# The first three feature blocks behind two layer norms, taken from unnormalized rows

## Chip, cores and metric

The kernel runs on one core of a Trainium2 chip. The metric is the device time of one execution in microseconds (us), and the time of a kernel is the median of its runs. PE is TensorE's matmul stream and PEld its weight loads, DVE is VectorE, ACT is ScalarE, POOL is GpSimd, SP is SyncE, which issues the weight transfers.

## What is computed

Two transformer blocks follow each other on 256 tokens of width 1024. The change touches the two places where a layer norm stands ahead of a wide product:

```python
x = layer_norm(ALPHA * x + gate1 * mixed, ln1_g[l], ln1_b[l])
h2 = x * (1.0 + scale2) + shift2
y_ffn = peer_ffn(h2, ...)              # begins with q = h2 @ w_query, 1024 x 2048
x = layer_norm(ALPHA * x + gate2 * y_ffn, ln2_g[l], ln2_b[l])
...
hn = rms_norm_2(x, norm_mix_g[0])      # second block
gate, xr = split(hn @ w_in)            # rglru_mixer, 1024 x 2048
gate = gelu(gate)
```

`layer_norm` is `(x - mean) / sqrt(var + eps) * g + b` over the 1024 features of a token. I call the two places the first norm (ahead of the query product, line L351 from 419.76 us) and the second norm (ahead of the recurrent mixer, from 1259.79 us).

## The kernel before

Activations are held feature-major: a tile `[128, 8, 256]` has 8 chunks of 128 features, with the 256 tokens along the free dimension. Every product is made in fp32 accuracy from split operands: a value is cast to `hi` (ACT, type fp32r), and `lo = value - hi` (DVE); a product takes the three matmuls hi·hi, hi·lo and lo·hi. A weight block of 1024 x 128 arrives by a transfer of SP's queue into one of four `raw` buffers, is cast to `whi` by ACT (L234) and split to `wlo` by DVE (L235). `whi` and `wlo` come from a ring of three pairs, so the cast of block n+3 waits until the matmuls of block n are over. `K.deepen` adds a second ring of three pairs; it is not there around the first norm.

One output block of 128 features is 24 matmuls (8 chunks x 3), in the function `ws` (L279 to L281). The first three blocks behind a norm are made together by `ws_wave` (L351 to L353): 72 matmuls, ordered so that chunk k of the first block comes ahead of chunk k-1 of the second, which lets the wave begin when only the first chunks are normalized.

The class `LayerNorm` works in three steps. `pair(j, acc)` is called as each pair of chunks leaves the product ahead of the norm: it updates the residual `x` (L939), squares it (ACT), and adds up sums and sums of squares (DVE, POOL). `stats` sums over the partitions with one-column matmuls against `ones` (L965), forms the negated mean and the reciprocal deviation on 128x2 tiles (L966 to L972), and spreads each over 128 partitions by two matmuls into PSUM, `B[0]` and `B[1]` (L989). `center` and `norm` (L978, L983) then subtract and multiply two chunks at a time. Behind them the caller splits the normalized rows: at the first norm ACT makes `xhi` (L906), DVE makes `h` again in fp32 (L907) and DVE or POOL subtract (L909); ACT also writes the residual `x<-x,cols` (L912). At the second norm ACT makes `xhi` (L1286), the residual (L1289) and squares for the RMS norm (L1305), and DVE makes `xlo` (L1290) and adds the squares (L1307). `Residual.factors` turns these sums into `rsB`, the RMS factor.

The order on each engine is fixed when the program is built: a scheduler places instructions by their place in the program and by when it thinks that their inputs are ready. On the chip ACT, DVE and POOL take their lists strictly in that order.

Behind the first norm the query blocks are numbered c0 to c15. c0 to c2 are the wave, c3 is the first one by `ws`; each block's `scores` (L1052, tile `psc`) follow, from the copy `R` of the block that ACT makes (L1082). Behind the second norm the wave makes three gate blocks, and x0, x1, x2, x3 (tile `xr`) are the first blocks by `ws`; DVE takes them from PSUM (`xs`, L1389) and runs a convolution (`xc`, L1391, L1393).

Of the kernel before, what the change touches and what calls it, by code (L numbers as in the profile page):

```python
# [10 lines left out]
F32 = mybir.dt.float32  # L11
# [368 lines left out]
def new_x(k):  # L380
    hi = k.xop.tile([P, 8, T], F32R, tag="hi", name=k.nm("xhi"))
    lo = k.xop.tile([P, 8, T], F32R, tag="lo", name=k.nm("xlo"))
    return hi, lo


def setup(k):
# [11 lines left out]
    k.mod = c.tile([P, 48], F32, name="mod")  # L398
    k.skT = c.tile([P, 2, P], F32, name="skT")
# [57 lines left out]
def block1_mixers(k):  # L457
# [6 lines left out]
    def sl(name, shape, dt=F32):  # L464
        return slab.tile(shape, dt, tag="s", name=k.nm(name))
# [450 lines left out]
    return fm(hhi), fm(hlo)  # L916


class LayerNorm:
# [3 lines left out]
    def __init__(self, k, x, gate, scale, work, st):  # L923
        nc = k.nc
        self.k, self.x, self.st = k, x, st
        self.sum, self.sq, self.q = work[:, 0], work[:, 1], [work[:, 2], work[:, 3]]
        self.gate = st[:, 16:24]
        nc.vector.tensor_scalar(self.gate, gate, scale / ALPHA, None, op0=OP.mult)
# [5 lines left out]
    def pair(self, j, acc):  # L934
# [9 lines left out]
        add = nc.vector.tensor_add  # L944
        if j in (1, 2):
            add(self.sum, self.sum if j == 2 else self.two(0), self.two(j))
            nc.gpsimd.tensor_add(self.sq, self.sq, q)
            if j == 2:
                nc.gpsimd.tensor_add(self.sq[:, :T], self.sq[:, :T], self.sq[:, T:])
        S, Q = self.sum[:, :T], self.sq[:, :T]  # L950
        if j == 3:
            add(S, S, self.sum[:, T:])
            add(S, S, x[:, 6])
            with self.k.tc.issue_after(add(S, S, x[:, 7]).ins):
                add(Q, Q, q[:, :T])
            add(Q, Q, q[:, T:])

    def stats(self):
# [51 lines left out]
def peer(k, X, finish):  # L1010
# [227 lines left out]
class Residual:  # L1238
# [6 lines left out]
    def start(self):  # L1245
# [23 lines left out]
        self.ln = LayerNorm(k, self.x, k.mod[:, 40:], 1.0, wk, slab.take(24))  # L1269
# [108 lines left out]
def rglru(k, res, X):  # L1378
    nc = k.nc
    with k.tc.tile_pool(name="rg", bufs=1) as slab, k.tc.tile_pool(name="rgw", bufs=2) as work:  # L1380
# [63 lines left out]
        ps = [k.mm("gt") for _ in range(3)]  # L1444
        k.ws_wave([p[:, :T] for p in ps], X)
# [3 lines left out]
        for f in range(3):  # L1449
            gt(f, ps[f])  # L1450
# [335 lines left out]
def program(tc, A, out):  # L1786
    with ExitStack() as es:
# [24 lines left out]
```

## Time and profile before

| | |
|---|---|
| median of 3 runs | 1856.93 us (1855.01 to 1860.98) |
| profiled execution, its own time | 1854.88 us |
| span of the profile | 1853.2 us |
| busy share of PE, DVE, ACT, POOL | 97%, 76%, 51%, 13% |
| matmuls of L351 to L353 at the first norm | from 419.76 to 430.27 us |
| the same at the second norm | from 1259.79 to 1270.31 us |

The span is the profiled part of one execution; its own time is 1.7 us longer. A profile row of the timeline gives the start and the length of an instruction on an engine, and in brackets how long that engine had been idle and what released it. The granted clock is a share of TensorE's full 2.4 GHz; 0.50 is the lower level, 1.2 GHz.

### The profile page before, as it was taken

To read this page: it belongs to the slowest core of one execution; us is meant where nothing else is said; L and a number is where in the kernel's file an instruction comes from. 1 tells how busy PE (TensorE), PEld (TensorE's weight loads), DVE (VectorE), ACT (ScalarE), POOL (GpSimd) and SP (SyncE) were. 2 spreads that over 40 slices of the span, in tenths; PEclk is the share of its full clock that TensorE was granted. 3 is DMA by queue.
4 is the path that set the end of the run, shared out by engine and by line. 5 is a ranking of instruction groups with operands and counts; after the bars stand their busy time and mean duration, and the time that the engine had idled before them with its cause. 6 is when DMAs were issued, how large, how long until landed. Compare 5 with 4: busy or idle time off the path is not lost.

```text
span 1853.2 us, 36938 instructions
## 1 busy us (share of the span) xinstructions
PE 1803.7 (97%) x14795; PEld 1719.7 (93%) x14795; DVE 1400.2 (76%) x2487; ACT 945.2 (51%) x1603; POOL 248.9 (13%) x273
## 2 busy tenths in 40 slices
PE   8999999989999999999999999998899999999998
PEld 6987899989999999999999999998789999788997
DVE  6998977878898977777888765568975556876554
ACT  3776765445445444444444544457754445664443
POOL 1000230010021300000000000001722222322221
PEclk9999999999999999999999999998999999999999
DMA  9666546874566555555555665664458666216662
GB/s 361 212 211 202 161 160 212 300 239 144 164 186 188 175 180 170 163 169 164 167 169 162 197 193 183 184 203 126 126 188 289 194 185 193 81 61 201 187 187 91
DMA packets 91150, 339.61 MB, mean 183 GB/s; under 512 B 10257, under 2 KB 10433, under 8 KB 89570
## 3 DMA queue, kind: packets, MB, share of 16 engines
q1 hardware_dynamic: 87794, 322.01, 55.3%
q0 software_dynamic: 2752, 14.54, 2.3%
q8 instruction: 116, 1.90, 0.4%
q10 hardware_dynamic: 432, 0.70, 0.1%
q14 instruction: 56, 0.46, 0.1%
HBM read 335.06 MB, written 5.30 MB: 184 GB/s over the span
## 4 chain that ended last, share of the span: by engine, by line
PE 81%; DVE 7%; DMA 6%; ACT 3%; issue 2%; POOL 0%; POOLq 0%; ACTq 0%; SPq 0%; DVEq 0%
PE u L279 7%; PE pv L320 7%; PE u L280 7%; PE u L281 7%; PE pv L322 7%; PE pv L321 7%; PE md L301 5%; PE up L281 3%; PE up L280 3%; PE up L279 3%; DVE wlo L235 2%; PE g L1183 2%; PE md L322 2%; PE md L321 2%; PE md L320 2%
## 5 line engine op out<-in xcount | busy, mean ns | idle before, releaser
L234 ACT CAST whi<-raw 128x1024 fp32r<-128x1024 f32 x525 | 547.8, 1045 | 529.3 <-PE u L280 196.2
L235 DVE TENSOR_TENSOR wlo<-raw,whi 128x1024 fp32r<-128x1024 f32 x525 | 662.6, 1264 | 205.1 <-ACT whi L234 202.8
L279 PE MATMUL u<-xhi,whi 128*128 128x256 f32 x1024 | 292.5, 286 | 0.0
L280 PE MATMUL u<-xlo,whi 128*128 128x256 f32 x1024 | 289.5, 283 | 0.0
L281 PE MATMUL u<-xhi,wlo 128*128 128x256 f32 x1024 | 289.5, 283 | 0.0
L320 PE MATMUL pv<-wh,whi 128*128 128x256 f32 x1000 | 285.4, 285 | 0.0
L321 PE MATMUL pv<-wh,wlo 128*128 128x256 f32 x1000 | 282.7, 283 | 0.0
L322 PE MATMUL pv<-wl,whi 128*128 128x256 f32 x1000 | 282.7, 283 | 0.0
L280 PEld LDWEIGHTS u<-xlo,whi 128*128 128x128 f32 x1024 | 196.3, 192 | 0.0
L279 PEld LDWEIGHTS u<-xhi,whi 128*128 128x128 f32 x1024 | 196.3, 192 | 0.0
L281 PEld LDWEIGHTS u<-xhi,wlo 128*128 128x128 f32 x1024 | 196.2, 192 | 0.0
L321 PEld LDWEIGHTS pv<-wh,wlo 128*128 128x128 f32 x1000 | 191.7, 192 | 0.0
L320 PEld LDWEIGHTS pv<-wh,whi 128*128 128x128 f32 x1000 | 191.7, 192 | 0.0
L322 PEld LDWEIGHTS pv<-wl,whi 128*128 128x128 f32 x1000 | 191.6, 192 | 0.0
L357 ACT ACTIVATE wh<-P 128x256 fp32r<-128x256 f32 x128 | 53.2, 417 | 199.5 <-PE pv L321 197.9
L281 PE MATMUL up<-xhi,wlo 128*128 128x256 f32 x464 | 131.5, 283 | 0.0
L279 PE MATMUL up<-xhi,whi 128*128 128x256 f32 x464 | 131.0, 282 | 0.3 <-DVE r L1481 0.3
L280 PE MATMUL up<-xlo,whi 128*128 128x256 f32 x464 | 131.3, 283 | 0.0
L1483 POOL TENSOR_TENSOR r<-r 128x256 f32<-128x256 f32 x64 | 75.7, 1185 | 262.3 <-ACT hh L1482 262.3
L358 DVE SCALAR_TENSOR_TENSOR wl<-P,wh 128x256 fp32r<-128x256 f32 x128 | 54.3, 424 | 63.7 <-ACT wh L357 63.7
L279 PEld LDWEIGHTS up<-xhi,whi 128*128 128x128 f32 x464 | 87.7, 189 | 1.6 <-DVE r L1481 0.5
L280 PEld LDWEIGHTS up<-xlo,whi 128*128 128x128 f32 x464 | 87.4, 188 | 1.2
(601 smaller groups left out, 4411.1 us busy)
## 6 DMA issues: line engine op xcount, KB each, us to landing
raw<-in_peer_u SPq DMA_DIRECT2D x128, 512.0 KB, 3.6
raw<-in_peer_v SPq DMA_DIRECT2D x128, 512.0 KB, 3.6
raw<-in_w_up SPq DMA_DIRECT2D x64, 512.0 KB, 4.2
raw<-in_w_down SPq DMA_DIRECT2D x64, 512.0 KB, 3.9
raw<-in_w_in_a SPq DMA_DIRECT2D x33, 512.0 KB, 4.1
raw<-in_ada SPq DMA_DIRECT2D x32, 512.0 KB, 4.6
raw<-in_w_in_b SPq DMA_DIRECT2D x32, 512.0 KB, 3.7
ada<-in_ada SPq DMA_DIRECT2D x8, 1024.0 KB, 12.6
```

Source lines behind the costliest of these rows:

```text
L234: nc.scalar.copy(hi, raw)
L235: self.marks.append(nc.vector.tensor_sub(lo, raw, hi.bitcast(F32)))
L279: mm(out, hi[:, s], xh(kk), start=kk == 0, stop=False)
L280: mm(out, hi[:, s], xl(kk), start=False, stop=False)
L281: mm(out, lo[:, s], xh(kk), start=False, stop=kk == nk - 1)
L301: mm(acc[2 * tc + h], x(k)[:, s], v[:, h * 512:h * 512 + 512], start=st, stop=sp)
L320: mm(o, hi[:, s], xh(k), start=f and h == 0, stop=False)
L321: mm(o, lo[:, s], xh(k), start=False, stop=False)
L322: mm(o, hi[:, s], xl(k), start=False, stop=l and h == 1)
L357: self.nc.scalar.activation(hi, full, AF.Copy, scale=scale)
L358: self.nc.vector.scalar_tensor_tensor(lo, full, scale, hi.bitcast(F32), op0=OP.mult, op1=OP.subtract)
L1483: nc.gpsimd.tensor_mul(r, r, r)
```

## The change

The first three blocks are now multiplied from rows that are not yet normalized. `pair` also splits `x * w` into `raw` tiles (`rhi`, `rlo` at the first norm, `xhi`, `xlo` at the second), where w is the product of the gains behind the norm; two extra columns of the raw tile hold w itself and the shift b. `head` runs the 72 matmuls on these tiles, 258 columns wide (tile `hd`), and `headed` corrects each block: it copies the two extra columns of the result (tile `hw`), adds negated mean times the first of them, multiplies by the reciprocal deviation `B[1]`, and the caller adds the second. The chunk sums over the partition are no longer folded on DVE and POOL first: `stats` uses 16 one-column matmuls in place of 4. The remaining blocks (c3 onwards, x0 onwards) still use normalized rows. At the first norm `h` moves from DVE to ACT, and all four subtractions go to DVE. At the second norm the normalized rows get tiles of their own, `x0hi` and `x0lo`.

```diff
-    ln = LayerNorm(k, xt, mod[:, 16:24], 0.5, lns, lst)
+    ln = LayerNorm(k, xt, mod[:, 16:24], 0.5, lns, lst, [sl(n, [P, 8, T + 2], F32R) for n in ("rhi", "rlo")],
+                   gl[:, :8], gl[:, 8:])
...
+    ln.head(3)
     with k.tc.high_priority():
         ln.stats()
...
-        for i in range(2):
-            f = 2 * j + i
+        fs = 2 * j, 2 * j + 1
+        for f in fs:
             nc.scalar.activation(hhi[:, f], xt[:, f], AF.Identity, scale=g(f), bias=b(f))
-            nc.vector.tensor_scalar(h[:, i], xt[:, f], g(f), b(f), op0=OP.mult, op1=OP.add)
-        e = nc.gpsimd if j % 2 else nc.vector
-        e.tensor_sub(hlo[:, 2 * j:2 * j + 2], h, hhi[:, 2 * j:2 * j + 2].bitcast(F32))
+        for f in fs:
+            nc.scalar.activation(h[:, f % 2], xt[:, f], AF.Identity, scale=g(f), bias=b(f))
+        nc.vector.tensor_sub(hlo[:, 2 * j:2 * j + 2], h, hhi[:, 2 * j:2 * j + 2].bitcast(F32))
...
+        for f in (2 * j, 2 * j + 1):
+            hi, lo = [v[:, f, :T] for v in self.raw]
+            w = self.w[:, f:f + 1]
+            nc.scalar.activation(hi, x[:, f], AF.Copy, scale=w)
+            nc.vector.scalar_tensor_tensor(lo, x[:, f], w, hi.bitcast(F32), op0=OP.mult, op1=OP.subtract)
...
+    def head(self, n):
+
+        self.ps = [self.k.mm("hd") for _ in range(n)]
+        self.k.ws_wave([p[:, :T + 2] for p in self.ps], (lambda i: self.raw[0][:, i], lambda i: self.raw[1][:, i]))
+
+    def headed(self, i, tmp, nm):
+
+        nc = self.k.nc
+        if i == 0:
+            nc.scalar.copy(nm, self.B[0][:, :T])
+        ps = self.ps[i]
+        c = self.hw[:, 2 * i:2 * i + 2]
+        nc.scalar.copy(c, ps[:, T:T + 2])
+        nc.vector.scalar_tensor_tensor(tmp, nm, c[:, 0:1], ps[:, :T], op0=OP.mult, op1=OP.add)
+        nc.vector.tensor_mul(tmp, tmp, self.B[1][:, :T])
+        return c[:, 1:2]
...
-        for i, u in enumerate((self.sum, self.sq)):
-            for tc in range(2):
-                nc.tensor.matmul(ps[:, i * 2 + tc:i * 2 + tc + 1], u[:, tc * P:tc * P + P], k.ones, start=True, stop=True)
+        q = self.q[1]
+        parts = [[self.sum[:, :T], self.sum[:, T:], self.x[:, 6], self.x[:, 7]],
+                 [self.sq[:, :T], self.sq[:, T:], q[:, :T], q[:, T:]]]
+        n = 0
+        for b in range(4):
+            for i in range(2):
+                for tc in range(2):
+                    nc.tensor.matmul(ps[:, i * 2 + tc:i * 2 + tc + 1], parts[i][b][:, tc * P:tc * P + P], k.ones,
+                                     start=n == 0, stop=n == 15)
+                    n += 1
...
+    nm = sub(T)
     for c in range(16):
+        q = qT[c % 2]
         if c > 2:
...
-        nc.scalar.copy(qT[c % 2], pq[c][:, :T])
+            nc.scalar.copy(q, ps[:, :T])
+        else:
+            nc.scalar.activation(q, q, AF.Identity, bias=head.headed(c, q, nm))
...
         for f in range(3):
-            gt(f, ps[f])
+            c = res.ln.headed(f, gate[:, f], res.ln.sum[:, :T])
+            nc.vector.scalar_tensor_tensor(gate[:, f], gate[:, f], c, res.rsB, op0=OP.add, op1=OP.mult)
```

The change moves instructions on every engine. The first place is ACT's list at the first norm, from the square root of the deviation (L971 before, L1000 now) to the first casts of query weights; `whi_4931` before and `whi_4970` now belong to block c3, `x<-x,cols` is the residual. Before:

```order
L971 ACTIVATE lnst<-lnst 128x2
L906 ACTIVATE xhi_4778<-x_3917,gl 128x256 x2
L912 ACTIVATE x_3917<-x_3917,cols 128x256 x2
...
L912 ACTIVATE x_3917<-x_3917,cols 128x256 x2
L234 CAST whi_4931<-raw_4929 128x1024
L234 CAST whi_4937<-raw_4935 128x1024
L234 CAST whi_4943<-raw_4941 128x1024
L1082 COPY R<-q_4842 128x256
```

and of the change, on the same engine at the same place:

```order
L1000 ACTIVATE lnst<-lnst 128x2
L909 ACTIVATE xhi_4882<-x_3918,gl 128x256 x2
L911 ACTIVATE h_4887<-x_3918,gl 128x256 x2
...
L915 ACTIVATE x_3918<-x_3918,cols 128x256 x8
L976 COPY hw<-hd_4777 128x2
L976 COPY hw<-hd_4778 128x2
L976 COPY hw<-hd_4779 128x2
L234 CAST whi_4970<-raw_4968 128x1024
L234 CAST whi_4976<-raw_4974 128x1024
L234 CAST whi_4982<-raw_4980 128x1024
L973 COPY R<-lnB_4853 128x256
L234 CAST whi_4988<-raw_4986 128x1024
L1113 ACTIVATE R<-R,hw 128x256 x2
```

Between the root and the cast for c3 stood 16 activations of 128x256, and 24 and three small copies stand there now; the rows `R` of c0 and c1, which the scores need, stand behind the cast for c6.

The second place is ACT's list at the second norm, from the root (L971, L1000) to the first normalized chunks; `whi_16050` before is the weight of a later block (x4), and now `whi_16100` is that of x0 and `whi_16130` that of x4. Before:

```order
L971 ACTIVATE res<-res 128x2
L234 CAST whi_16050<-raw_16048 128x1024
L1286 ACTIVATE xhi_15859<-res 128x256 x2
L1289 ACTIVATE res<-res,cols 128x256 x2
L1286 ACTIVATE xhi_15859<-res 128x256
```

and of the change:

```order
L1000 ACTIVATE res<-res 128x2
L976 COPY hw<-hd_15906 128x2
L234 CAST whi_16100<-raw_16098 128x1024
L234 CAST whi_16130<-raw_16128 128x1024
L1318 ACTIVATE x0hi<-res 128x256 x2
L1321 ACTIVATE res<-res,cols 128x256 x2
```

A copy from the first block of the product and a second weight cast now stand ahead of the first normalized chunk.

The third place is DVE's list at the second norm, from the negated mean (L966, L995) to the reciprocal; `wlo` is a weight split, `xlo_13681` is `lo` of the raw rows. Before:

```order
L966 TENSOR_SCALAR res<-lns_15841 128x2
L968 TENSOR_TENSOR res<-res 128x2
L969 SCALAR_TENSOR_TENSOR res<-lns_15841,res 128x2
L970 TENSOR_SCALAR res<-res 128x2
L972 RECIPROCAL res<-res 128x2
```

and of the change:

```order
L995 TENSOR_SCALAR res<-lns_15981 128x2
L959 SCALAR_TENSOR_TENSOR xlo_13681<-res,xhi_13680 128x256
L997 TENSOR_TENSOR res<-res 128x2
L959 SCALAR_TENSOR_TENSOR xlo_13681<-res,xhi_13680 128x256
L998 SCALAR_TENSOR_TENSOR res<-lns_15981,res 128x2
L235 TENSOR_TENSOR wlo_16119<-raw_16116,whi_16118 128x1024
L999 TENSOR_SCALAR res<-res 128x2
L1001 RECIPROCAL res<-res 128x2
```

Two splits of raw rows and one weight split have come between the mean and the deviation.

## Rows read from the trace of the kernel before

**Rows 1.** The page: span, and the chain that ended last by engine.

```profile
span 1853.2 us, 36938 instructions
...
PE 81%; DVE 7%; DMA 6%; ACT 3%; issue 2%; POOL 0%; POOLq 0%; ACTq 0%; SPq 0%; DVEq 0%
```

**Rows 2.** Stretches at the first norm: length, busy time by engine, clock, DMA.

```profile
410.90:414.00 3.10, 0.00 (x0) 0.00 (x1) 3.03 (x7) 0.75 (x2) 1.97 (x2) 0.86 0.01 3
...
420.00:422.00 2.00, 2.00 (x9) 1.81 (x10) 2.00 (x5) 2.00 (x5) 0.00 (x0) 0.50 0.00 0
422.00:424.00 2.00, 2.00 (x13) 2.00 (x13) 2.00 (x5) 1.90 (x5) 1.33 (x2) 0.65 0.00 0
...
440.00:445.00 5.00, 5.00 (x44) 5.00 (x44) 5.00 (x21) 1.79 (x4) 0.00 (x0) 1.00 0.55 189
```

**Rows 3.** Timeline of PE at the first norm.

```profile
410.60 0.28 PE L322 MATMUL wo<-xlo,w 128*128 128x256 f32 x1
...
414.00 1.94 PE L965 MATMUL lns<-ones,lns 128*128 128x1 f32 x8 [3.12 <-DVE lns L954]
...
419.76 0.58 PE L351 MATMUL q<-xhi,whi 128*128 128x256 f32 x1 [1.32 <-ACT xhi L906]
...
430.15 0.28 PE L353 MATMUL q<-xlo,whi 128*128 128x256 f32 x1
430.27 0.28 PE L279 MATMUL q<-xhi,whi 128*128 128x256 f32 x1
...
431.03 0.39 PE L281 MATMUL q<-xhi,wlo 128*128 128x256 f32 x1 [0.36 <-DVE wlo L235]
...
441.85 0.61 PE L1052 MATMUL psc<-skT,R 128*128 128x128 f32 x4
```

**Rows 4.** Timeline of ACT at the first norm.

```profile
419.11 1.09 ACT L906 ACTIVATE xhi<-x,gl 128x256 fp32r<-128x256 f32 x2 [2.14 <-DVE x L983]
...
426.22 1.08 ACT L912 ACTIVATE x<-x,cols 128x256 f32<-128x256 f32 x2
428.67 3.08 ACT L234 CAST whi<-raw 128x1024 fp32r<-128x1024 f32 x3 [1.37 <-PE q L353]
```

**Rows 5.** Timeline of POOL and DVE at the first norm.

```profile
410.70 1.38 POOL L947 TENSOR_TENSOR lns<-lns 128x512 f32<-128x512 f32 x1 [0.29 <-ACT lns L943]
411.00 1.37 DVE L952 TENSOR_TENSOR lns<-lns 128x256 f32<-128x256 f32 x1
...
413.08 0.41 DVE L953 TENSOR_TENSOR lns<-lns,x 128x256 f32<-128x256 f32 x1
...
415.98 0.16 DVE L966 TENSOR_SCALAR lnst<-lns 128x2 f32<-128x2 f32 x1 [1.17 <-PE lns L965]
...
418.66 0.75 DVE L983 TENSOR_TENSOR x<-x,lnB 128x256 f32<-128x256 f32 x2
```

**Rows 6.** Timeline of PE at the second norm.

```profile
1248.63 0.28 PE L322 MATMUL pv<-wl,ahead 128*128 128x256 f32 x1
...
1259.79 0.58 PE L351 MATMUL gt<-xhi,whi 128*128 128x256 f32 x1 [2.05 <-ACT xhi L1286]
...
1270.31 0.95 PE L1316 MATMUL rs<-ones,res 128*128 128x1 f32 x8
```

**Rows 7.** Timeline of ACT at the second norm.

```profile
1259.13 1.09 ACT L1286 ACTIVATE xhi<-res 128x256 fp32r<-128x256 f32 x2
...
1268.71 0.63 ACT L1305 ACTIVATE res<-res 128x512 f32<-128x512 f32 x1
```

**Rows 8.** Timeline of DVE behind the second norm.

```profile
1256.29 0.17 DVE L972 RECIPROCAL res<-res 128x2 f32<-128x2 f32 x1 [0.27 <-ACT res L971]
...
1275.87 0.42 DVE L1389 TENSOR_TENSOR xs<-xr,res 128x256 f32<-128x256 f32 x1
```

**Rows 9.** Stretches in the recurrent mixer, columns as in rows 2.

```profile
1288.00:1292.00 4.00, 4.00 (x36) 4.00 (x35) 3.01 (x5) 3.22 (x6) 3.69 (x5) 1.00 0.48 135
...
1296.00:1300.00 4.00, 4.00 (x36) 4.00 (x35) 4.00 (x5) 2.31 (x5) 2.88 (x3) 1.00 0.50 149
...
1304.00:1308.00 4.00, 0.41 (x2) 0.21 (x2) 4.00 (x6) 1.90 (x4) 2.33 (x3) 0.93 0.37 130
```

More of the change, by code (lines that the diff above doesn't have):

```diff
@@ L377, in fm, with new_x @@
     return lambda k: t[:, k, :]
[L380 to L383, printed above, removed]
+def new_x(k, wide=False):
+    x = [k.xop.tile([P, 8, T + 2], F32R, tag=n, name=k.nm("x" + n)) for n in ("hi", "lo")]
+    return x if wide else [v[:, :, :T] for v in x]
 def setup(k):
@@ L915, in block1_mixers, with __init__ @@
     es.close()
-    return fm(hhi), fm(hlo)
+    return ln, (fm(hhi), fm(hlo))
 class LayerNorm:
-    def __init__(self, k, x, gate, scale, work, st):
+    def __init__(self, k, x, gate, scale, work, st, raw, w, b):
         nc = k.nc
+        self.hw = k.hw
         self.k, self.x, self.st = k, x, st
@@ L927, in __init__ @@
         self.gate = st[:, 16:24]
+        self.raw, self.w = raw, w
+        hi, lo = raw
+        for c, v in ((T, w), (T + 1, b)):
+            nc.scalar.copy(hi[:, :, c], v)
+            nc.vector.tensor_sub(lo[:, :, c], v, hi[:, :, c].bitcast(F32))
         nc.vector.tensor_scalar(self.gate, gate, scale / ALPHA, None, op0=OP.mult)
@@ L943, in pair @@
             nc.scalar.activation(q, self.two(j), AF.Square)
-        add = nc.vector.tensor_add
+        for f in (2 * j, 2 * j + 1):
[3 more added lines that the diff above has]
+            nc.vector.scalar_tensor_tensor(lo, x[:, f], w, hi.bitcast(F32), op0=OP.mult, op1=OP.subtract)
         if j in (1, 2):
-            add(self.sum, self.sum if j == 2 else self.two(0), self.two(j))
+            nc.vector.tensor_add(self.sum, self.sum if j == 2 else self.two(0), self.two(j))
             nc.gpsimd.tensor_add(self.sq, self.sq, q)
[L948 to L956, printed above, removed]
+    def head(self, n):
[11 more added lines that the diff above has]
+        return c[:, 1:2]
     def stats(self):
@@ L1007, in take, with peer @@
         return a
-def peer(k, X, finish):
+def peer(k, head, X, finish):
     nc, A = k.nc, k.A
@@ L1075, in peer @@
     top = gen_top()
-    pq = [k.mm("q") for _ in range(3)]
-    k.ws_wave([ps[:, :T] for ps in pq], X)
+    nm = sub(T)
     for c in range(16):
+        q = qT[c % 2]
         if c > 2:
-            pq.append(k.mm("q"))
-            k.ws(pq[c][:, :T], X)
-        nc.scalar.copy(qT[c % 2], pq[c][:, :T])
+            ps = k.mm("q")
+            k.ws(ps[:, :T], X)
+            nc.scalar.copy(q, ps[:, :T])
+        else:
+            nc.scalar.activation(q, q, AF.Identity, bias=head.headed(c, q, nm))
         if c:
@@ L1268, in start, with first @@
         nc.gpsimd.tensor_scalar(nl, hc, -1.0, None, op0=OP.mult)
-        self.ln = LayerNorm(k, self.x, k.mod[:, 40:], 1.0, wk, slab.take(24))
+        self.ln = LayerNorm(k, self.x, k.mod[:, 40:], 1.0, wk, slab.take(24), new_x(k, True), self.gl[:, :8], self.gl[:, 8:])
         ahead = [ahead.tile([P, 2, 1024], F32R, name=k.nm("ahead")) for _ in range(3)]
         return self.ln, [(w[:, 0], w[:, 1]) for w in ahead]
-    def first(self):
+    def first(self, pool):
         k, nc, x = self.k, self.k.nc, self.x
+        self.ln.head(3)
         with k.tc.high_priority():
@@ L1278, in first @@
             self.ln.center(0)
-        hi, lo = new_x(k)
+        hi, lo = [pool.tile([P, 8, T], F32R, name=n) for n in ("x0hi", "x0lo")]
         for j in range(4):
@@ L1735, in block2 @@
 def block2(k, res):
-    X = res.first()
     with k.tc.tile_pool(name="t5", bufs=1) as pool:
         t5 = t5_load(k, pool)
-        X = rglru(k, res, X)
+        with k.tc.tile_pool(name="x0", bufs=1) as xp:
+            X = rglru(k, res, res.first(xp))
         X = mlp(k, res, X, 0, lambda: t5_start(k, res, *t5))
@@ L1790, in program @@
         k.plan = plan_block1(k) + plan_block2(A)
-        X = block1_mixers(k)
+        ln, X = block1_mixers(k)
         res = Residual(k)
-        peer(k, X, res.start)
+        peer(k, ln, X, res.start)
         block2(k, res)
```

6 lines of the change are left out of this document (3 added, 3 removed).

## Prediction

> **What bounds the kernel now.** I read the page's chain first: PE holds 81% of it [rows 1], so a change pays only where PE waits. The stretches show where. Late in the query product PE is busy 5.00 of 5.00 us with 44 matmuls, 0.114 us each, at clock 1.00 [rows 2]; there nothing is to be had, and a delay handed to this stretch stays in the time. At the first norm it is otherwise: between 410.90 and 414.00 PE does nothing, and in 420 to 422, at clock 0.50, DVE and ACT are both busy 2.00 of 2.00 while the wave's matmuls follow the chunks [rows 2]. The timeline gives the ends of the hole: the product ahead ends at 410.72 (the matmul at 410.60 with a matmul's 0.12), the wave begins at 419.76, ends at 430.27, and only 0.36 is lost behind it [rows 3]. The second norm is the same shape: 1248.75 to 1259.79, wave over at 1270.31 [rows 6]. Behind it the bound changes: in the recurrent mixer DVE is busy 3.01 of 4.00, then 4.00 of 4.00, and by 1304 to 1308 PE does 0.41 of 4.00 [rows 9].
>
> **The first norm: the product.** It now starts at 410.72 in place of 419.76. Its 72 matmuls are 8.6 at 0.12. (The two columns more, the copies of the columns and the small casts cost under 0.2 and lie beside this work.) The statistics' matmuls stand among them: 16, which make 32 rows of the timeline for the 8 before; the 8 took 1.94 cold [rows 3], and 8 of the same form took 0.95 warm at the second norm [rows 6], so 0.12 each, 3.8. The spreads are 8 more rows, at 0.15 (0.61 for 4 warm score rows [rows 3]) 1.2. PE also waits about 1.2 for the sums and squares of the last pair: POOL's add of 1.38 starts at 410.70, and DVE's 1.37 and 0.41 run to 413.49 [rows 5]; bounds 0 and 2.8, and I take 1.2 because seven products stand ahead of the first sum. Sum 14.8: the product ends near 425.6, 4.7 earlier than before.
>
> **The first norm: what c3 waits for.** c3 needs normalized rows and its own weights. By the order the last statistics matmul stands behind 23 products: 410.72 + 2.8 + 3.8 + 1.2 = 418.5, and the mean can start at 418.9, 2.9 later than its 415.98 [rows 5]. One raw split (at 0.41, as the like add in [rows 5]) has come in between on DVE, and I let half of it, 0.2, delay the chain. So the multiplication by the deviation (418.66 [rows 5]) and ACT's first normalized chunk behind it (419.11 [rows 4]) move by 3.1, the latter to 422.2. On ACT stood 16 activations, 419.11 to 427.30 [rows 4], 0.51 each; now there are 24 (eight for `h`), 12.2, and three small copies, 0.5: ACT is free at 434.9. Only then comes the weight cast for c3, which in the kernel before ran at 428.67 and led to c3's third matmul at 431.03 [rows 3, 4], 2.36 later. So that matmul is at 437.3, **+6.3**. This is the stall that replaces the removed one: from 425.6 to about 436 PE has nothing that it may do (the last normalized chunk is ready near 431). What is queued behind the cast on ACT is every later weight cast and the copies `R`; the scores of c0 and c1 wait for those.
>
> In so long a pause the clock falls: before, it stood at 0.50 in 420 to 422 and 0.65 in the next stretch [rows 2]. c3's 22 remaining matmuls (2.6 warm) then run partly at 1.2 GHz: between 0 and 2.6 more, I take **+1.2**, about half, because before the level came back only within 422 to 424, at least 2 us after the wave's begin [rows 2, 3]. c3 then ends at 441.1. The cast for c6 waits until c3 gives its ring pair back (1.03, a third of 3.08 [rows 4]), and the rows `R` of c0 and c1 stand behind it (0.54 each, half of 1.08 [rows 4]): 443.2. c4 covers most of that; small waits of the scores remain, **+0.6** (0 to 2.0). What PE had done at 441.85 + 0.61 [rows 3] is so done 6.3 + 1.2 + 0.6 = **8.1** later, and the full stretch behind it keeps the delay. If the statistics come no later than before (-3.1) and the clock costs nothing, it is 3.8; with the long waits 9.5.
>
> **`h` on ACT.** DVE loses eight instructions at 0.40 (5 in 2.00 [rows 2]), 3.2, and ACT gains eight at 0.51, 4.1. In 420 to 422 both engines are full [rows 2], and ACT also issues the casts that PE waits for, so I count the 4.1 (it is inside the +6.3) and give nothing for the 3.2. The Trainium skill ("Perfetto Trace Analysis", section "Optimizing Scalar/DVE Operations") says that with a saturated DVE, offloading work to ScalarE may make sense; by that the term would be a gain, and it becomes a rival below. The trace shows DVE saturated as the page supposes, but ACT as well.
>
> **The second norm.** The reciprocal ended at 1256.46 [rows 8]. The statistics' 24 more rows at 0.12 are 2.9, the dropped fold (1.37 + 0.41 and a hand-over of 0.3 [rows 5]) returns 2.1: mean +0.8. Ahead of the reciprocal DVE now has two raw splits (0.84 at 0.41 [rows 5]) and one weight split (at most 431.03 - 428.67 - 1.03 = 1.3 [rows 3, 4]): reciprocal about 1259.3. Its spread stands behind 58 products: 1248.75 [rows 6] + 7.0 + 3.8 + the waits of 1.2 = 1260.8. ACT must then take a copy from the first block (over at about 1261.1), and two weight casts (2.06): the first `x0hi` is at 1263.2 in place of 1259.13 [rows 7], **+4.1**. The 20 ACT instructions that follow took 10.2 (1259.13 to 1268.71 + 0.63 [rows 7]), so x0's rows are complete near 1273.4. PE finishes the product at 1262.9, in place of 1270.31 [rows 6], and then follows x0's chunks at ACT's pace until 1273.9: four blocks, where three were over at 1270.31 and the fourth would be at 1273.2. PE is thus even within 1 (2.4 if the clock falls).
>
> DVE decides instead. `xs` of x0, which stood at 1275.87 [rows 8], is late by 4.1, and by six more corrections at 0.42 (2.5); one weight split (1.3) is done ahead rather than behind: +5.3, `xs` near 1282. The mixer behind is bound by DVE [rows 9], and its slack is 1.0 (3.01 of 4.00): **+4**. Bounds: 0, if DVE's later idle time takes all, and 5.5, with no slack.
>
> **Sum.** 8.1 + 4.0 = 12.1. The profiled execution took 1854.88 and would take 1867.0; it lies 2.05 below the median of 1856.93, so I predict 1869. The case's own bounds are 3.8 + 0 and 9.5 + 5.5: 1860.7 to 1871.9. A change under 0.3% (5.6 us, 1851.4 to 1862.5) is what a measurement here could not tell from none.
>
> **Rivals.**
> - *Both holes are closed, with nothing behind.* PE gains 4.7 at the first norm and 7.4 at the second (1270.31 - 1262.9): 12.1, 1845. It decides if ACT delivers c3's cast by 423.2 (2.36 ahead of 425.6) and x0's chunks early. For it: the holes are real, 9 and 11 us. Against: 24 activations alone are 12.2 and cannot start before the deviation. Chance 0.10.
> - *DVE was the pace, and relieving it pays.* Then the eight activations are free (8.1 - 4.1) and normalization is 3.2 shorter: +0.8, with the second norm's +4 it is 1861.7. It needs ACT to finish 24 activations in the time of 16, 0.34 each; its rows are 0.51 [rows 4], without gaps to fill in 420 to 422. This is the mechanism of the skill's offloading rule, and the full ACT in this trace speaks against it. Chance 0.10.
> - *The mixer takes the second delay up.* Only the first norm's 8.1 is left, 1865; with the first at its low bound 1860.7. For it: 1.0 of idle DVE time every 4 us at the beginning. Against: 4.00 of 4.00 later [rows 9]. Chance 0.14, of which 0.04 within 0.3%.
> - *The cold clock spreads.* After the second pause x1 to x3 run at half clock too (72 matmuls, up to 8.6 more), of which half reaches DVE: about 1873.5. Chance 0.10.
>
> **How the numbers follow.** The forecast keeps 0.56. Slower holds 0.56 + 0.10 + 0.10 = 0.76, the same 0.10 + 0.04 = 0.14, faster 0.10. The range leaves out the first rival and the far end of the last: 1858 to 1876; the likeliest case's own is 1861 to 1872.
>
> **What would show it.** Right: the product's last matmul near 425.6 and 1262.9; PE idle from there to about 436 with a low granted clock; ACT's cast for c3 near 435; first `x0hi` near 1263, first `xs` near 1282. Wrong: a cast for c3 before 430 (then the product's gain is kept), 24 activations in under 9 us, or a mean at 416 in spite of the products ahead of it.

## The result, and the profile after

The changed kernel takes 1871.12 us (median of 4 runs, 1870.23 to 1873.88) where the kernel before takes 1855.97 (median of 4, 1854.70 to 1860.98, one run more than in the table ahead): ratio 1.0082, interval 1.0069 to 1.0096, so it is slower by 15.2. The forecast was 1869.0 in a range of 1858 to 1876. The profiled execution of the changed kernel is the slowest of its four (1873.88, span 1872.2), and the one of before lies 1.1 under its median. Sums made from the two profiles therefore come to 19.0, some 4 more than the medians differ.

PE's timeline of the changed kernel, first norm, then second (columns as in [rows 3]):

```profile
411.21 0.28 PE L351 MATMUL hd<-rhi,whi 128*128 128x258 f32 x1
...
413.89 0.61 PE L992 MATMUL lns<-ones,lns 128*128 128x1 f32 x4 [1.68 <-DVE lns L961]
...
415.42 2.72 PE L992 MATMUL lns<-ones,lns 128*128 128x1 f32 x12 [0.46 <-POOL lns L962]
...
418.57 0.42 PE L351 MATMUL hd<-rhi,whi 128*128 128x258 f32 x1
...
423.50 0.85 PE L992 MATMUL lns<-ones,lns 128*128 128x1 f32 x4
...
433.10 0.28 PE L353 MATMUL hd<-rlo,whi 128*128 128x258 f32 x1
...
441.97 0.58 PE L279 MATMUL q<-xhi,whi 128*128 128x256 f32 x1 [8.59 <-ACT whi L234]
...
455.10 0.61 PE L1081 MATMUL psc<-skT,R 128*128 128x128 f32 x4
...
1254.51 0.28 PE L351 MATMUL hd<-xhi,whi 128*128 128x258 f32 x1
...
1273.95 0.28 PE L353 MATMUL hd<-xlo,whi 128*128 128x258 f32 x1
```

The product starts at once behind the one ahead (411.21; the whole norm is 0.49 later than in [rows 3]), but takes 22.0 us and not the 8.6 of its 72 matmuls. PE then idles 8.59 for ACT's cast for c3. The score row that stood at 441.85 [rows 3] stands at 455.10. At the second norm the product takes 19.6, from 1254.51 to 1274.07; before, the 72 matmuls ran from 1259.79 to 1270.31 [rows 6], behind a product that ended 5.8 earlier.

The stretches say why the product is slow; one more belongs to the long products in the middle, and the last to the time behind the second norm (columns as in [rows 2]; the numbers in brackets behind a busy time count instructions):

```profile
412.00:414.00 2.00, 0.32 (x3) 0.12 (x2) 1.97 (x5) 1.25 (x3) 0.12 (x2) 1.00 0.00 0
414.00:416.00 2.00, 1.54 (x10) 1.33 (x10) 2.00 (x5) 0.99 (x3) 1.36 (x1) 0.82 0.00 0
416.00:418.00 2.00, 2.00 (x11) 2.00 (x11) 0.43 (x2) 0.81 (x2) 0.00 (x0) 0.50 0.00 0
426.00:428.00 2.00, 2.00 (x12) 2.00 (x10) 1.29 (x2) 0.00 (x0) 0.00 (x0) 0.50 0.04 8
...
1100.00:1200.00 100.00, 100.00 (x846) 100.00 (x845) 58.09 (x71) 47.49 (x70) 0.00 (x0) 1.00 0.60 185
...
1280.00:1282.00 2.00, 1.41 (x7) 1.11 (x6) 1.64 (x4) 2.00 (x6) 0.00 (x0) 0.50 0.71 229
```

In 412 to 414 PE did little (0.32 of 2.00), then one-column rows among the products; by 416 the clock is at 0.50 and stays there through 428, with PE busy all of the time and 10 to 12 matmuls in 2 us. 26 of the 72 matmuls of the product have the length of 0.42 or more that the row at 418.57 shows (418.00 to 428.64), and 20 at the second norm; nearly all others take 0.28. In 416 to 418 DVE, ACT and POOL are busy only 0.43, 0.81 and 0.00: what is left waits for the mean, and the mean waits for a statistics matmul that stands behind cold products. DVE's and ACT's timelines (as in [rows 4, 5, 7, 8]):

```profile
424.38 0.16 DVE L995 TENSOR_SCALAR lnst<-lns 128x2 f32<-128x2 f32 x1 [7.95 <-PE lns L992]
...
1266.45 0.16 DVE L995 TENSOR_SCALAR res<-lns 128x2 f32<-128x2 f32 x1 [6.92 <-PE lns L992]
...
1294.29 0.42 DVE L1421 TENSOR_TENSOR xs<-xr,res 128x256 f32<-128x256 f32 x1
```

```profile
428.91 1.10 ACT L909 ACTIVATE xhi<-x,gl 128x256 fp32r<-128x256 f32 x2 [3.26 <-DVE x L1012]
...
440.87 2.94 ACT L234 CAST whi<-raw 128x1024 fp32r<-128x1024 f32 x3
444.16 0.38 ACT L973 COPY R<-lnB 128x256 f32<-128x256 f32 x1 [0.35 <-DMA x_scr<-x]
...
1273.99 1.09 ACT L1318 ACTIVATE x0hi<-res 128x256 fp32r<-128x256 f32 x2
```

The mean of the second norm in the kernel before, on DVE:

```profile
1255.26 0.16 DVE L966 TENSOR_SCALAR res<-lns 128x2 f32<-128x2 f32 x1 [1.17 <-PE lns L965]
```

The mean of the first norm is at 424.38 where it was at 415.98 [rows 5], ACT's first normalized chunk at 428.91 (419.11 [rows 4]), its casts at 440.87 (428.67 [rows 4]). At the second norm the mean is at 1266.45 (before 1255.26), `x0hi` at 1273.99 (1259.13 [rows 7]) and the first `xs` at 1294.29 (1275.87 [rows 8]).

To place the cost I take two differences in every kernel below. **N1** is the start of the score row at 441.85 [rows 3] less that of the last `wo` matmul (410.60). **N2** is the start of the mixer's last `xs` (before: 1308.4, in the view of that tile) less that of the last `pv` matmul (1248.63 [rows 6]). Against before, N1 is 12.8 longer in the changed kernel and N2 12.3. Together that is 25.1, while the span grew by 19.0. (Both come from one profiled execution of each kernel. In the kernels below whose norm is that of before, N1 lies from -1.2 to +0.7 and N2 from -0.2 to +1.0. In the three that have the changed second norm and nothing else new at it, N2 is +12.3, +10.5 and +9.1. So a difference under 2 in N1 or under 3 in N2 means little.) Between the norms something is given back: the 13.25 at the score row are 5.8 at the start of the second product (1254.51 against 1248.63 + 0.12). Nearly all of it is in the two long products, which the change doesn't touch: from their first weight load to their last they take 757.3 us and not 764.3. The stretch at 1100 shows it: 846 matmuls in 100 us, where the kernel before has 835, at the same clock:

```profile
1100.00:1200.00 100.00, 100.00 (x835) 100.00 (x834) 57.48 (x70) 46.77 (x70) 0.00 (x0) 1.00 0.61 185
```

### The profile page after: what moved, and what is told of

Read it like the earlier page. It is cut to its first block, busy times and chain, and to the rows that moved or that the text cites. A ratio compares the mean times of both kernels' runs of the same rounds, so it can differ in the third digit from the quotient of the medians.

```text
span 1872.2 us, 37063 instructions
## 1 busy us (share of the span) xinstructions
PE 1817.0 (97%) x14843; PEld 1732.4 (93%) x14843; DVE 1404.0 (75%) x2503; ACT 955.9 (51%) x1639; POOL 245.9 (13%) x269
## 4 chain that ended last, share of the span: by engine, by line
PE 70%; DVE 4%; ACT 2%; issue 1%; DMA 0%; POOL 0%; POOLq 0%; ACTq 0%; DVEq 0%
PE u L279 7%; PE pv L320 7%; PE u L281 7%; PE u L280 6%; PE pv L322 6%; PE pv L321 6%; PE md L301 5%; PE up L281 3%; PE up L280 3%; PE up L279 3%; PE g L1214 2%; PE md L320 2%; PE md L322 2%; PE md L321 1%; DVE wlo L235 1%
```

## The experiments

Times are medians; the ratio in brackets, with its interval, is to the kernel before on the same chip.

| kernel | time, ratio | N1, N2 against before |
|---|---|---|
| the change | 1871.12 (1.0082, 1.0069 to 1.0096) | +12.8, +12.3 |
| first norm only | 1858.52 (1.0018, 1.0007 to 1.0028) | +11.9, +0.3 |
| second norm only | 1856.52 (1.0004, 0.9994 to 1.0014) | -1.2, +10.5 |
| wide tiles only | 1846.93 (0.9956, 0.9941 to 0.9970) | +0.7, +1.0 |
| statistics last | 1871.96 (1.0093, 1.0073 to 1.0114) | +12.2, +10.1 |
| statistics last, rows moved | 1868.68 (1.0067, 1.0053 to 1.0082) | +11.8, +10.1 |
| residual write on DVE | 1865.91 (1.0056, 1.0041 to 1.0072) | +8.0, +9.1 |
| mean early | 1861.64 (1.0030, 1.0018 to 1.0041) | +6.2, +4.7 |
| mean early, all edits | 1859.02 (1.0017, 1.0007 to 1.0026) | +8.8, +6.1 |
| pad of 32 bytes | 1852.81 (0.9981, 0.9972 to 0.9990) | |
| pads on both sides | 1849.22 (0.9957, 0.9945 to 0.9970) | |
| pad of 160 bytes | 1843.91 (0.9933, 0.9920 to 0.9947) | |
| wide tiles and far pad | 1844.04 (0.9931, 0.9918 to 0.9945) | |

**The change at one norm only.** At the other norm the code of before is used again, with all tiles as in the change. For the first norm only, this is the core:

```diff
-        self.ln = LayerNorm(k, self.x, k.mod[:, 40:], 1.0, wk, slab.take(24), new_x(k, True), self.gl[:, :8], self.gl[:, 8:])
+        self.ln = LayerNorm(k, self.x, k.mod[:, 40:], 1.0, wk, slab.take(24))
...
-            c = res.ln.headed(f, gate[:, f], res.ln.sum[:, :T])
-            nc.vector.scalar_tensor_tensor(gate[:, f], gate[:, f], c, res.rsB, op0=OP.add, op1=OP.mult)
+            gt(f, ps[f])
```

> Only the first norm is changed; behind the second norm everything is as in the kernel before. In the changed kernel's profile the work behind the first norm is 12.6 us later than before (last score rows 12.9 later, 0.3 to 0.5 of it older), and then 7.1 us are given back between 475 and 1250 us, where matmuls follow each other every 0.119 us and in the kernel before every 0.120. Theory A, the norm costs 12.6 and the quicker stretch belongs to the changed kernel's memory layout (tiles 258 wide): about +5.5 us over before, and scores again 12 to 13 us late. Theory B, the forecast's sum (+8.1 at this norm, the quicker stretch is an accident of one execution): +8, scores 8 to 13 late. If the stretch is an accident and the norm costs 12.6: +12.6.

> Only the second norm is changed; the first one works as before. In the changed kernel's profile the last xs is 12.2 us further behind than the end of the product ahead of the norm. Theory A (this norm costs 12.2, the layout gives 7 back): +5 us. Theory B (the forecast's +4.0 at this norm): +4, the last xs 4 later. If the norm costs 12.2 and the quicker stretch was an accident: +12.

Either half costs ten or more in its own place, yet neither moves the total by more than 2.7. So something in both halves gives about as much back. (Both came out lower than either expectation: +2.6 and +0.6.)

**Only the tiles.** The kernel before, with tiles as wide as the change makes them and none of its work:

```diff
-    hi = k.xop.tile([P, 8, T], F32R, tag="hi", name=k.nm("xhi"))
-    lo = k.xop.tile([P, 8, T], F32R, tag="lo", name=k.nm("xlo"))
-    return hi, lo
+    x = [k.xop.tile([P, 8, T + 2], F32R, tag=n, name=k.nm("x" + n)) for n in ("hi", "lo")]
+    return [v[:, :, :T] for v in x]
...
+    k.hw = c.tile([P, 8], F32, name="hw")
...
-        return slab.tile(shape, dt, tag="s", name=k.nm(name))
+        t = slab.tile([P, 8 * (T + 2)], dt, tag="s", name=k.nm(name))[:, :math.prod(shape[1:])]
+        return t if len(shape) == 2 else t.rearrange("p (a b) -> p a b", a=shape[1])
```

> The kernel before, with the same instructions in the same order, only its xhi and xlo tiles and the big buffers 258 columns wide instead of 256 (256 are used). Theory A, the layout sets the pace of the long products: 6 to 9 us faster than before, matmuls every 0.119 us between 480 and 1240 us. Theory B, the pace is an accident of an execution: within 2 us of before, with no fixed pace.

It is 9.0 faster than before, as theory A has it, and its stretch has the faster pace:

```profile
1100.00:1200.00 100.00, 100.00 (x845) 100.00 (x844) 58.09 (x71) 47.52 (x70) 0.00 (x0) 1.00 0.61 186
```

So the layout, not the early product, is what gives time back: by the weight loads 7.1 in the two long products; where the rest lies isn't shown. (The tile `hw` of the edit is also 32 bytes that move what lies behind it; such a pad alone is tried below.) Against this kernel the first norm costs 11.6 by the medians (1858.52 - 1846.93), the second 9.6, both 24.2. The 3.0 that they cost together beyond the sum is about the width of the intervals, and I leave it open.

**Statistics behind the product.** All 16 one-column matmuls wait for the last of the 72:

```diff
-        for b in range(4):
...
+        with k.tc.issue_after(self.mms[at - 1].ins):
+            for b in range(4):
```

> The changed kernel with the 16 one-column matmuls of both norms issued behind all 72 matmuls of the product, instead of one pair after every three matmuls or so. Theory A, waiting for the sums and the one-column matmuls in between hold the clock at 0.50 and stretch the product: the product runs at full clock from 411.2 to about 420, the mean is formed near 424 (424.4 in the changed kernel), so nothing is lost by the later place, the casts for c3 to c5 stand ahead of the normalization in ACT's order, and c3 follows the chunks: its end near 437 instead of 446, 8 us less at the first norm, several us at the second: 10 to 16 us faster than the changed kernel, about equal to before. Theory B, the chain over ACT alone sets the end and the place of the statistics does not matter: the mean comes 3 or more us later and the time is that of the changed kernel or more.

The stretches of this kernel at the first norm, then at the second:

```profile
412.00:414.00 2.00, 2.00 (x19) 2.00 (x18) 2.00 (x3) 0.17 (x1) 1.52 (x1) 1.00 0.25 100
414.00:416.00 2.00, 2.00 (x17) 1.93 (x17) 1.97 (x5) 1.44 (x3) 0.59 (x1) 1.00 0.00 0
416.00:418.00 2.00, 1.92 (x15) 1.70 (x15) 1.93 (x4) 1.24 (x4) 0.86 (x1) 1.00 0.00 0
...
1262.00:1266.00 4.00, 4.00 (x38) 4.00 (x36) 1.24 (x2) 3.18 (x6) 0.00 (x0) 0.98 0.77 223
1266.00:1270.00 4.00, 3.71 (x16) 3.33 (x16) 1.48 (x4) 2.33 (x2) 0.00 (x0) 0.50 0.36 128
```

and rows of PE's, DVE's and ACT's timelines of the same kernel:

```profile
421.41 1.84 PE L995 MATMUL lns<-ones,lns 128*128 128x1 f32 x16
...
446.38 0.55 PE L279 MATMUL q<-xhi,whi 128*128 128x256 f32 x1 [6.13 <-DVE R L979]
...
1263.65 4.84 PE L995 MATMUL lns<-ones,res 128*128 128x1 f32 x32
```

```profile
425.07 0.16 DVE L998 TENSOR_SCALAR lnst<-lns 128x2 f32<-128x2 f32 x1 [2.92 <-PE lns L995]
425.15 1.23 DVE L235 TENSOR_TENSOR wlo<-raw,whi 128x1024 fp32r<-128x1024 f32 x1
426.30 0.15 DVE L1000 TENSOR_TENSOR lnst<-lnst 128x2 f32<-128x2 f32 x1
426.37 1.22 DVE L235 TENSOR_TENSOR wlo<-raw,whi 128x1024 fp32r<-128x1024 f32 x1
```

```profile
445.30 0.37 ACT L975 COPY R<-lnB 128x256 f32<-128x256 f32 x1 [2.40 <-DMA x_scr<-x]
```

The product now takes 9.1, near the forecast's 8.6: clock 1.00, over by 421.41. The first 16 of the 32 statistics rows take 1.84, 0.115 each. The time stays, as theory B has it. The mean comes hardly earlier, 12.8 behind the product's start (425.07 against 412.27; 13.2 in the change), and now two weight splits stand between it and the deviation. And a second wait appears: c3 is done early, but the next block's PSUM bank is free only when the first block has gone to `R`, and the first write to `R` waits for a transfer of the residual (`x_scr<-x`); of PE's 6.13, 2.40 are that wait, the rest goes to ACT's list ahead of it and to the correction behind it. At the second norm the 32 thin rows alone took 4.84, and while they ran the clock went from 0.98 to 0.50, with PE busy 4.00 of 4.00 before.

**The same, with the first rows of `R` elsewhere.** To take that wait away, `qT` and `nm` were put at another place of `R`:

```diff
-    qT = [sub(T) for _ in range(2)]
+    qT = [R[:, 12384 + i * T:12384 + i * T + T] for i in range(2)]
...
-    nm = sub(T)
+    nm = R[:, 12384 + 2 * T:12384 + 3 * T]
```

> The run with the statistics behind the product, and the rows R of c0 to c2 (and of every later block) and the spread mean moved within R to a place that covers no tile in use at the norm, where before they covered the residual x that is still to be written out. In the run before this one PE stood idle 6.13 us (440.3 to 446.4) for the correction that writes R, which waited for the transfer of x. Theory A (the gain of the early product was eaten by this wait): the wait goes, c4 follows c3 at 440.3, 6 us less than that run, about 1866, and 5 less than the changed kernel. Theory B (ACT's chain ends as late anyway): the wait moves to the weight cast or the scores and the time stays near 1871.

```profile
442.08 0.55 PE L279 MATMUL q<-xhi,whi 128*128 128x256 f32 x1 [6.69 <-DVE R L979]
```

The wait stayed, so the edit didn't do what it was for, and the 3.3 less than in the kernel above are no evidence: N1 is shorter by 0.4 only, and the last `wo` matmul alone is 3.8 earlier (408.33 and 412.16). (ACT's copy shows the same 2.40 idle until `x_scr<-x`.)

**The residual write on DVE.** The eight activations at L915 go from ACT to DVE; the change's `h` stays on ACT:

```diff
-        nc.scalar.activation(xt[:, f], xt[:, f], AF.Identity, scale=k.col("ln1g", f), bias=k.col("ln1b", f))
+        nc.vector.tensor_scalar(xt[:, f], xt[:, f], k.col("ln1g", f), k.col("ln1b", f), op0=OP.mult, op1=OP.add)
```

> The changed kernel with the eight writes of the residual at the first norm on DVE, which idles from 437.6 us, in place of ACT. Nothing else. Theory A (the forecast's step: the cast for c3 stands behind 24 activations on ACT, and each of them costs PE its length): ACT is free at 436.8 instead of 440.8, c3's first matmul comes at 438 instead of 441.97: 4 us less than the changed kernel, 1867. Theory B (the transfer of x and the rows R end last): c3 comes earlier but c4 or the scores wait for R until about 442 to 444: 1 to 2 us less.

ACT's and PE's timelines of this kernel (its last `wo` matmul is at 409.03):

```profile
425.10 1.09 ACT L909 ACTIVATE xhi<-x,gl 128x256 fp32r<-128x256 f32 x2 [2.54 <-DVE x L1012]
...
433.13 2.94 ACT L234 CAST whi<-raw 128x1024 fp32r<-128x1024 f32 x3
438.31 0.37 ACT L973 COPY R<-lnB 128x256 f32<-128x256 f32 x1 [2.23 <-DMA x_scr<-x]
```

```profile
434.23 0.58 PE L279 MATMUL q<-xhi,whi 128*128 128x256 f32 x1 [4.94 <-ACT whi L234]
```

c3 starts 25.2 behind the last `wo` matmul and no longer 30.9, and N1 is 4.8 shorter. Of those 5.7, 3.9 are ACT's list: from the first normalized chunk to the cast for c3 it takes 8.0 (425.10 to 433.13) where it took 12.0 (428.91 to 440.87). The other 1.8 came ahead of the list, where the edit changes nothing. So the length of ACT's list was a price, as forecast, of some 4 for these eight. N2 is 3.2 shorter too, although the second norm is untouched, so the total's 5.2 isn't the edit's alone. The Trainium skill ("Perfetto Trace Analysis", section "Optimizing Scalar/DVE Operations") says that with a saturated DVE it may make sense to move work to ScalarE. Here the other direction paid: the cast that PE waits for stands in ACT's list, and in the changed kernel DVE wasn't saturated there, it idled 4.33 ahead of the split for c3.

**The mean early.** The folds of before and its 4 statistics matmuls come back, ahead of the raw splits on DVE, and the matmuls stand behind at least 28 products:

```diff
+            with self.k.tc.high_priority():
+                self.up = nc.vector.scalar_tensor_tensor(x[:, f], acc[:, s], self.gate[:, f:f + 1], x[:, f], op0=OP.mult, op1=OP.add)
...
+        with k.tc.issue_after(self.mms[at - 1].ins):
+            for i, u in enumerate((self.sum, self.sq)):
...
+                    nc.tensor.matmul(ps[:, i * 2 + tc:i * 2 + tc + 1], u[:, tc * P:tc * P + P], k.ones, start=True, stop=True)
```

> The changed kernel with the mean formed early again: sums are folded on DVE and POOL as in the kernel before (4 statistics matmuls in place of 16), the residual updates of each pair stand ahead of the raw splits on DVE, and the statistics stand behind 35 products. Casts, h and the residual write are as in the changed kernel. Theory A (the late mean, 8.4 us at the first norm and 5 behind its distance in the kernel before at the second, is what the forecast mis-sized, and everything behind it follows it): the mean is formed near 417 instead of 424.4, the clock stays at 1.00 through the product, the cast for c3 comes at 433 instead of 440.9: 7 to 8 us at the first norm, 5 to 7 at the second, about 1857. Theory B (the waits behind it take it up, because the transfer of x and DVE in the mixer end last anyway): less than 5 us, 1866 or more.

Stretches, and rows of DVE and PE, of this kernel:

```profile
416.00:418.00 2.00, 0.97 (x9) 0.76 (x8) 1.97 (x7) 0.25 (x1) 0.00 (x0) 1.00 0.00 0
418.00:420.00 2.00, 2.00 (x18) 2.00 (x18) 0.86 (x4) 0.00 (x0) 0.00 (x0) 1.00 0.00 0
...
1276.00:1278.00 2.00, 2.00 (x10) 2.00 (x10) 1.17 (x5) 0.26 (x1) 0.00 (x0) 0.50 0.00 0
```

```profile
419.47 0.16 DVE L1001 TENSOR_SCALAR lnst<-lns 128x2 f32<-128x2 f32 x1 [1.07 <-PE lns L1000]
...
1257.10 0.14 DVE L1001 TENSOR_SCALAR res<-lns 128x2 f32<-128x2 f32 x1
```

```profile
435.59 0.58 PE L279 MATMUL q<-xhi,whi 128*128 128x256 f32 x1 [11.29 <-ACT whi L234]
```

The mean comes 7.2 behind the product's start (412.3), 6.0 sooner than in the change, and N1 is 6.6 shorter. At the second norm it comes 3.8 sooner (8.1 behind the start against 11.9), the first `x0hi` 5.9 sooner (13.6 against 19.5), and N2 is 7.6 shorter than in the change (4.4 than in the lowest of the three with the same second norm). So the way to the mean, with the cold products on it, was paid in full at the first norm; at the second the shorter DVE list counts as well, and the edit doesn't part the two. Nor does it part the clock from the number of statistics matmuls. What is left at the first norm, 6.2, has the forecast's mechanism: PE idles even longer ahead of c3, 11.29, because the product ends early and ACT's list is as long as it was. What is left at the second, 4.7, holds a cold stretch that the sum left out: behind the product PE runs at clock 0.50 again, from 1266 to 1280, as the stretch at 1276 shows. The time, 9.5 under the change, lies between the two theories.

**All edits together.** Mean early, the residual write on DVE, the cast for c3 ahead of the root, the copies `hw` behind the activations, the first rows of `R` elsewhere, a pad of 32 bytes on the far side:

```diff
+        self.k.later = []
+        self.k.fetch(1)
+        self.late, self.k.later = self.k.later, None
...
+            with self.k.tc.issue_after(self.acts[-1].ins):
+                nc.scalar.copy(nm, self.B[0][:, :T])
```

> The early mean, and c3's weight cast ahead of the square root on ACT, the copies of the extra columns behind the normalized chunks, the residual write on DVE, and the second ring moved by 32 bytes. Theory A (the chain product, mean, normalized rows, casts is what costs; with its waits gone the head start of the product is left): below the kernel with wide tiles alone, 1840 to 1847. Theory B (the copies R and so the fifth block's bank wait for the transfer of x, which cannot be earlier than in the kernel before, and DVE bounds the mixer): PE waits for R near 436 and nothing is gained over the wide tiles: 1847 to 1856.

```profile
424.68 1.05 ACT L235 CAST whi<-raw 128x1024 fp32r<-128x1024 f32 x1 [7.30 <-PE hd L363]
```

```profile
442.69 0.55 PE L288 MATMUL q<-xhi,whi 128*128 128x256 f32 x1 [4.22 <-DVE R L1005]
```

The cast moved forward takes a ring pair that c0 still uses: ACT idles 7.30 for c0's matmuls, the root stands behind it, and N1 is longer than with the mean early alone (8.8 against 6.2). PE then also waits 4.22 for `R`. The gain in the total over that kernel, 2.6, isn't at the norms, and 1859.02 lies above what either theory expected.

**Where the tiles lie.** Four kernels, all from the kernel before without the change. A pad of 32 bytes; the same and one at the far end; the same and 128 bytes more ahead of `xhi`; and the wide tiles with the far pad:

```diff
+    k.pad = c.tile([P, 8], F32, name="pad")
...
+    k.padr = k.es.enter_context(k.tc.tile_pool(name="padr", bufs=1, side="right")).tile([P, 8], F32, name="padr")
...
+    k.padx = k.xop.tile([P, 32], F32, tag="pad", name="padx")
```

(The first kernel has the first line, the second the first two, the third the first and the last, the fourth the second line and the edit of the wide tiles.)

> The kernel before with one unused 32-byte tile ahead of the weight ring, and nothing else: all tiles keep their width, the ring's tiles start at 36224 in place of 36192 bytes of a partition (whi), a multiple of 64 instead of one of 32 only. Theory A, the place of the weight ring against 64 bytes sets the pace of the long products: all of the gain of the wide tiles (1846.9 against 1855.9, 9 us), matmuls every 0.119 us between 480 and 1240. Theory B, the row width of 258 columns spreads the reads: no gain, 1856.

> As the one before, and another unused 32-byte tile at the far end of the memory, so that the second ring of weights (165344 to 165312), the residual and the buffers of the second block start at multiples of 64 bytes as well. Theory A (the place of the rings): the second block has 2,700 matmuls of width 256 in the first product of each MLP and 1,100 in the second, half of whose weights lie in the second ring; at 0.001 us each and less for the rest it gains another 2 to 5 us over the first pad. Theory B (something else in the first block): no more than the first pad.

> The kernel before with unused tiles of 32 bytes ahead of the weight ring and 128 bytes ahead of xhi. All tiles have their 256 columns, and everything behind xhi and xlo (the tiles P, wh, wl of the two long products) starts at the same byte as in the kernel with wide tiles. Theory A (where wh, wl and the others start decides the pace of the long products): 0.119 us per matmul between 480 and 1240, 7 us faster there, 1848. Theory B (the width of the rows of xhi does): 0.120, and 1853 like the kernel with the 32-byte tile alone. If only one of the two products is quicker, it is 3.6.

> The kernel before with the wide tiles (8.9 us faster) and the unused 32 bytes at the far end (another 4 us where it was tried beside the first pad). No other change: the same instructions in the same order. If the two gains lie in different stretches, as the profiles say (the long products of the first block, the MLPs of the second), they add up: 12 to 13 us less than before, 1843. If they are two readings of one gain: 1847.

The view of the tiles of the long products shows the weight loads (count, then the shortest, median and longest in ns, then the first and last start). The kernel before, the one with 32 bytes, the one with 160, and the wide tiles:

```profile
L279 PEld LDWEIGHTS u<-xhi,whi x1024: 187/192/193, 475.4 to 862.2; 128*128 128x128 f32 x171
...
L320 PEld LDWEIGHTS pv<-wh,whi x1000: 187/192/192, 862.6 to 1239.7; 128*128 128x128 f32 x167
```

```profile
L320 PEld LDWEIGHTS pv<-wh,whi x1000: 187/192/192, 863.3 to 1240.5; 128*128 128x128 f32 x167
```

```profile
L279 PEld LDWEIGHTS u<-xhi,whi x1024: 187/188/193, 475.2 to 859.5; 128*128 128x128 f32 x171
...
L320 PEld LDWEIGHTS pv<-wh,whi x1000: 187/188/193, 859.9 to 1233.5; 128*128 128x128 f32 x167
```

```profile
L320 PEld LDWEIGHTS pv<-wh,whi x1000: 187/188/193, 858.1 to 1231.7; 128*128 128x128 f32 x167
```

With 160 bytes `pv` takes 373.6 from its first load to its last and not 377.1, as with the wide tiles, and `u` 384.3 and not 386.8 (383.2 with the wide tiles). The loads' median is 188 ns in place of 192 and a matmul starts every 0.1183 us at 845 in 100 us, in place of 0.1198 at 835. The wide tiles and the changed kernel have 188 too; the pads of 32 bytes have 192 and the old pace, and gain only in the second block's two MLPs (from the first `up` matmul of each to its last `md`, 3.6 less than before's 376.5 with one pad, 5.8 with two, 6.3 with 160 bytes, none with the wide tiles). So for `pv` wide rows aren't needed: a shift of the same rows does it, and 32 bytes don't; for `u` the shift gave 2.5 of 3.6. Neither theory had the 3.7 of the first pad, and with 160 bytes the time came out under both. Which tile's place and which rule is behind it, no run here tells. Far pad and wide tiles add up: the far pad is worth about 3.6 (7.3 with both pads, 3.7 with the first), the wide tiles 9.0, and the two together gave 11.8.

## Why the prediction was right, and where it was not

The time is right by luck, through two errors that nearly cancel: the norms cost 25.1 in the profiles, not 12.1, and the tiles' new places, for which the sum had no term, gave some 9 back. The direction and the stall behind ACT's list were foreseen, but the places in time that the prediction named as signs were missed: the product's end 433.2 (425.6 forecast), c3's cast 440.87 (435), and, less the 5.8 by which the second product starts later, its end 1268.3 (1262.9), the first `x0hi` 1268.2 (1263) and the first `xs` 1288.5 (1282; the terms given for it make 1281.2).

- *The clock in the product.* The sum put the 32 statistics rows at 0.12 each, 3.8, from a warm row of the second norm. They took 6.7 (0.61, 2.72 and four groups of 0.85), 2.9 more. Of the 72 matmuls 26 ran cold, one every 0.214 and not 0.12, 2.5 more. The waits for sums were 1.68 + 0.46 and not 1.2, the spreads 2 x 1.06 and not 1.2, 0.9 more each. Together that is the 7.2 by which 22.0 exceeds the forecast's 14.8. This is the step that failed: the sum looked for a cold clock only ahead of c3, and it came in the product, at both norms. (At the second the waits were 0.75 + 0.47, as forecast.) Whether the wait or the thin rows brought the clock down there, no run parts.
- *The mean.* +2.9 forecast, +8.4 in the rows, 7.9 without the later start; at the second norm +0.8 forecast, +5.4. The kernel with an early mean keeps the product at clock 1.00 and has norms that cost 10.9 (12.1 forecast), so what they cost beyond the forecast hangs on the way to the mean, at the second norm together with DVE's shorter list. The share of the clock in it is read from the rows, not tried by itself.
- *Mean to the first chunk.* 0.2 forecast; 4.53 where it was 3.13 [rows 4, 5], so 1.4, because the spread rows also stand behind cold products.
- *ACT's list.* 24 activations 12.2 forecast, 11.8 measured (428.91 to 440.72); the cast to c3's third matmul 2.36 as forecast (440.87 to 443.23). That ACT's list delays c3 was tried (residual write on DVE, 3.9 less on the list and N1 4.8 shorter).
- *The cold start of c3, and the scores.* +1.2 and +0.6 forecast; N1's 12.8 less the 11.7 by which c3's third matmul is later leaves 1.1 for both.
- *Behind the second mean.* To the first `x0hi` it took 3.7 longer than before (3.3 forecast), and from there to the first `xs` 3.6 longer (1.2 forecast); there PE ran at clock 0.50, in 1280 to 1292.
- *The mixer.* I let its slack take 1.3 of 5.3. It had 12.7 at the first `xs` and passes on 12.3 at the last. In the kernels with the second norm only and with the early mean it took up 2.1 (12.6 to 10.5, 6.8 to 4.7), so the slack taken lies between 0 and 2, and doesn't grow with the delay.
- *Rivals.* "Both holes are closed" fell: statistics behind the product did end the product by 421.41, and nothing was faster. "DVE was the pace" fell with ACT's rows: the 24 activations took 0.49 each, without a gap. The mixer didn't take the delay up. "The cold clock spreads" named the right cause, and came true in part where it said: some 40 of the 96 matmuls of x0 to x3 ran at half clock (1279.01 to 1292.31). It left out the product ahead.

Not in the prediction at all: that c4 needs a PSUM bank, the bank needs `R`, and `R` needs the residual's transfer. It stands so in the kernel before too, as ACT's timeline there shows:

```profile
432.35 0.65 ACT L1082 COPY R<-q 128x256 f32<-128x256 f32 x2 [0.60 <-DMA x_scr<-x]
```

A head start of the first three blocks can therefore carry PE only a few us past c3, whatever the statistics do; that this wait alone is the limit was argued from the releasers, not tried, since the edit meant to remove it didn't.

## What to carry to other kernels

Work that is moved ahead of a reduction must not stand in the way of the reduction: look at what the reduction's last matmul is queued behind, at the clock that the mixture of thin and wide matmuls leaves, and at the list of the engine that feeds the next stage. When a change alters the shape or the place of buffers, run a kernel with the buffers alone; here the buffers moved the time by as much as the change, in stages that it doesn't touch. The best kernels of this study leave the change out and move tiles: 1843.91 and 1844.04, 12 us under the kernel before.

## What the runs showed of the hardware

- The same matmuls at the same granted clock of 1.00 run at 835 or 845 in 100 us, with weight loads of 192 or 188 ns (median), as the tiles lie in SBUF: 6.0 of 764 us in two products with 160 bytes of padding, 7.1 with the wide tiles. With the MLPs' share the padded kernel is 12 of 1856 us faster.
- PE busy all of the time doesn't hold the clock by itself: 0.50 in 416 to 428 of the changed kernel, with one-column rows among the products, and 0.98 falling to 0.50 while 32 such rows ran alone (statistics last, second norm). At the first norm of that kernel the same 32 rows, from 421.41 to 425, left it at 1.00. A one-column row took 0.115 at the upper level and 0.21 at the lower.
- A gap of 1.03 in the busy time of one 2 us stretch, with 4 one-column matmuls in place of 16, left the clock at 1.00 (the kernel with the early mean).
